# The four query tiles of the opening attention head get a later planned landing time

## The chip, the cores and the metric

The kernel runs on one core of one Trainium2 chip. The metric is the device time in microseconds (us) of one execution. The profile names the engines: PE (TensorE matmul) with its weight loads PEld, DVE (VectorE), ACT (ScalarE), POOL (GpSimd) and SP (SyncE, which issues every DMA of this kernel; SPq is its queue).

## The reference, cut to what matters

One layer over 2048 prompt frames and 64 sample frames. An input projection (1024 to 6144 columns) gives queries, keys, values and gates of two branches; branch A is the differential attention in which the change lies:

```python
s = jnp.einsum('bqhcd,bkhcd->bhcqk', q, k).astype(jnp.float32) * (DK_A ** -0.5)
s = s - slopes[None, :, None, None, None] * dist[None, None, None]
s = jnp.where(allowed[None, None, None], s, -jnp.inf)
p = jax.nn.softmax(s, axis=-1)
a = p[:, :, 0] - lam * p[:, :, 1]
return jnp.einsum('bhqk,bkhe->bqhe', a.astype(v.dtype), v)
```

There are 4 heads. Branch B is a chunkwise retention. Both are normalised, gated, projected and added to the input.

## The kernel before, in words

**Stages.** The prompt is taken in two halves of 1024 frames. For each half the projection runs (the "w stream"), and while its later columns are still being multiplied, attention over that half runs beside it (the "z stream"): for each of 4 heads, and for each query tile of 256 frames (p = 0 to 3 in the first half, 4 to 7 in the second), scores Q K (lines 1879 and 1880), a mask and a minimum (1888), exponentials (1919), transposes (1991) and the product with V (1969 to 1971). Products are made of high and low float32r parts, which is why three matmuls stand where one would be expected. Retention blocks (2336 and on) run as a third stream.

**The order is planned by hand.** The Python program is itself a scheduler. `Hybrid.loop` holds a set of generators with priorities and a clock `self.pe`; each matmul moves this clock by its columns / 2.4 + 13 ns (`P`), and a generator that yields a time is resumed when the clock has reached it. PE, ACT and DVE execute their instructions in exactly the order in which the generators wrote them. The planned times are in no instruction: they only decide the order. Where the plan finds nothing to do, its clock jumps, and no instruction stands for the gap.

**Loads.** `ld` (line 279) issues a DMA on SP and returns the time at which the plan counts the data as landed: a running DMA clock that takes 1 ns for every 300 bytes, plus `DMA_LAT` = 2600 ns. A query tile is four DMAs of 131,072 bytes: 4 x 437 ns = 1.75 us on that clock; a weight tile of 262,144 bytes takes 0.87 us.

**The opening head.** `h_loader` calls `load_head(0, 0)`, which loads the two K tiles of head 0, its query tile p = 0, and, 3000 ns of the plan later, p = 1; 2000 ns after that the table `dfar`, and then V. The pool `q` has two buffers, so `q_loader` can load p = 2 only when p = 0 has been used, and p = 3 when p = 1 has; the load of p = 3 also waits until the K of head 1 is loaded (`self.heads` is not empty), `CALM` = 18000 ns after the end of `load_head(0, 0)`. `attn_head` takes the tiles in order and yields each one's planned landing time `tq` (line 1855) before it writes the scores. Line 1791 adds `FIRSTQ` = 4000 ns to the planned landing of tile p = 0 of head 0. All other query tiles count as landed when `ld` says so.

**What fills the wait.** While `attn_head` sleeps, lower priorities are written. At this place the w stream is in the first product of the second half (`transposed`, line 1426, with `mm_group`, line 1137): for two row tiles, two groups of 256 columns and two of 288, each group 8 steps of 3 matmuls; `mm_group` yields after each step. Then come the values of the second half (`natural`, 512 columns wide, 8 steps of 3 for each frame tile), whose weights pass from a load (`ws`) through a cast on ACT (`wh`, line 727) and a subtraction on POOL (`wl`, line 748).

Of the kernel before, what the change touches and what calls it, by code (L numbers as in the profile page):

```python
# [44 lines left out]
FIRSTQ = 4000.0  # L45
# [127 lines left out]
class Hybrid:  # L173
# [1595 lines left out]
    def load_head(self, half, h):  # L1769
        ap = self.ap  # L1770
        nu = half + 1
        ks = [[None] * nu for _ in range(2)]
        vs = [[None] * nu for _ in range(2)]
        tk = tv = 0
        for u in range(nu):
            usl = slice(1024 * u, 1024 * u + 1024)
            for c in range(2):
                yield from self.take("K")
                k = self.sb(ap, [128, 1024], "K", dt=F32R)
                for j in range(2):  # L1780
                    o = 64 * (j ^ c)
                    tk = self.ld(k[o:o + 64].bitcast(F32), self.kT[j][h, 64 * c:64 * c + 64, usl], 1 << 18)
                ks[c][u] = k
        hd = {"ks": ks, "vs": vs, "tk": tk, "tv": None}
        if self.far:
            self.heads.append(hd)
        else:
            self.far = True
            yield from self.load_q(0, 0)
            q, t = self.qs[0]  # L1790
            self.qs[0] = q, t + FIRSTQ
            yield self.pe + 3000
            yield from self.load_q(0, 1)
            yield self.pe + 2000
            self.ld(self.dfar, self.i["c_dfar"], 1 << 19)
            self.heads.append(hd)
        for u in range(nu):
            usl = slice(1024 * u, 1024 * u + 1024)
            for j in range(2):
                yield from self.take("V")  # L1800
                v = self.sb(ap, [128, 8, 128], "V", dt=F32R)
                tv = self.ld(v.bitcast(F32), self.vN[j][usl, 128 * h:128 * h + 128]
                             .rearrange("(t p) e -> p t e", p=128), 1 << 19)
                vs[j][u] = v
        hd["tv"] = tv

    def load_q(self, h, p):
        t0 = 256 * p
        yield from self.take("q")
        q = self.sb(self.ap, [128, 4, 256], "q", dt=F32R)  # L1810
        for j in range(2):
            qj = self.qT[j][h, :, t0:t0 + 256].rearrange("(c d) t -> d c t", c=2)
            for o in (0, 64):
                t = self.ld(q[o:o + 64, 2 * j:2 * j + 2].bitcast(F32), qj, 1 << 17)
        self.qs.append((q, t))

    def q_loader(self, half):
        for h in range(4):
# [1383 lines left out]
```

## Time and profile before

| | us |
|---|---|
| median of 3 runs | 1899.02 (1897.36 to 1899.72) |
| the profiled execution, device time | 1898.9 |
| its span, first to last instruction | 1897.1 |
| PE busy | 1872.0 |
| DVE, ACT, POOL busy | 1332.9, 972.9, 673.1 |
| mean granted TensorE clock | 0.999 |

A row of the timeline reads: start, length, engine, line, operation, output <- inputs, shapes, count, and in brackets how long the engine was idle just before and what released it. Matmuls overlap, so the length of one is more than the distance to the next. A row of the waits reads: who waited <- for whom: us in total, times, longest.

### The profile page before, as it was taken

The page shows a single profiled execution, that of the slowest core. Times are in us where ns is not written, and L with a number is a line of the kernel's source. Part 1 is how long each engine was busy: PE and PEld are TensorE (multiplying, and loading weights), DVE is VectorE, ACT ScalarE, POOL GpSimd, SP SyncE. Part 2 cuts the span into 40 slices and gives each one's busy share as a digit, 9 for nine tenths or more (in the row PEclk, how much of TensorE's full clock was granted, in tenths as well). Part 3 has the DMA queues.
Part 4 walks back from the last instruction along what each step waited for, and adds up shares of the span by engine and source line. Part 5 has one row for each costly group of instructions (what it writes and reads, how often), then busy time and mean ns, then how long its engine had stood idle before and what let it go on. Part 6 is the DMA issues. An engine that isn't in the chain of part 4 may idle for free.

```text
span 1897.1 us, 33035 instructions
## 1 busy us (share of the span) xinstructions
PE 1872.0 (99%) x11090; PEld 1648.1 (87%) x11090; DVE 1332.9 (70%) x3111; ACT 972.9 (51%) x2266; POOL 673.1 (35%) x729
## 2 busy tenths in 40 slices
PE   9999999999998999999999999999999999999999
PEld 7788778888887889888888899989999999999887
DVE  6765757657584777886467686588886869977664
ACT  6434544555434665655455565456666536654221
POOL 2420355555552122121311344332122546522442
PEclk9999999999999999999999999999999999999999
DMA  7664555666857867554622854945534899976542
GB/s 259 209 178 125 162 154 182 180 197 193 250 181 198 225 187 195 160 171 125 181 73 76 231 138 128 238 127 141 142 103 140 266 250 285 274 233 204 174 156 78
DMA packets 402556, 340.09 MB, mean 179 GB/s; under 512 B 85329, under 2 KB 348625, under 8 KB 401362
## 3 DMA queue, kind: packets, MB, share of 16 engines
q1 hardware_dynamic: 402386, 337.97, 61.0%
q8 instruction: 88, 1.44, 0.3%
q14 instruction: 82, 0.67, 0.1%
HBM read 218.27 MB, written 118.75 MB: 178 GB/s over the span
## 4 chain that ended last, share of the span: by engine, by line
PE 89%; DVE 4%; DMA 4%; SPq 1%; ACT 1%; issue 1%; POOL 0%; DVEq 0%; POOLq 0%; ACTq 0%
PE mm L1137 29%; PE mm L989 8%; PE tp L989 4%; PE at L1991 3%; PE s L1880 2%; PE s L1879 2%; PE s L989 2%; PE mm L1564 2%; PE pv L1971 2%; PE pv L1970 2%; PE pv L1969 2%; DMA q<-qT 1%; PE s L2793 1%; PE s L2795 1%; PE s L2794 1%; PE pv L2257 1%
## 5 line engine op out<-in xcount | busy, mean ns | idle before, releaser
L748 POOL TENSOR_TENSOR wl<-ws,wh 128x512 fp32r<-128x512 f32 x108 | 148.6, 1387 | 244.3 <-ACT wh L727 233.5
L1137 PE MATMUL mm<-wh,xh 128*128 128x512 f32 x504 | 203.7, 404 | 0.0
L1137 PE MATMUL mm<-wl,xh 128*128 128x512 f32 x504 | 197.8, 393 | 0.8 <-POOL wl L748 0.8
L1137 PE MATMUL mm<-wh,xl 128*128 128x512 f32 x504 | 198.2, 393 | 0.0
L1137 PE MATMUL mm<-xh,wh 128*128 128x288 f32 (+2 forms) x544 | 180.2, 331 | 0.0
L1137 PE MATMUL mm<-xl,wh 128*128 128x288 f32 (+2 forms) x544 | 176.1, 324 | 0.0
L1137 PE MATMUL mm<-xh,wl 128*128 128x288 f32 (+2 forms) x544 | 176.1, 324 | 0.0
L1919 ACT ACTIVATE row<-row,a_mx 128x1024 f32<-128x1024 f32 (+7 forms) x144 | 150.1, 1044 | 9.5 <-DVE a_mx L1898 9.5
L2007 DVE TENSOR_TENSOR atl<-at,ath 128x512 fp32r<-128x512 f32 (+1 forms) x144 | 93.1, 658 | 76.1 <-ACT ath L2005 75.6
L2005 ACT CAST ath<-at 128x512 fp32r<-128x512 f32 (+1 forms) x144 | 79.0, 564 | 108.0 <-PE at L1991 102.1
L856 POOL TENSOR_TENSOR wl<-ws,wh 128x256 fp32r<-128x256 f32 x64 | 54.5, 852 | 195.7 <-ACT wh L847 195.6
L1888 DVE CUSTOM_DVE_ANT_0 row<-s,dfar 128x512 f32<-128x512 f32 (+2 forms) x151 | 92.8, 629 | 38.1 <-PE s L1880 37.6
L1745 POOL TENSOR_TENSOR r_y<-r_y,r_sq 128x256 f32<-128x256 f32 x32 | 28.2, 881 | 253.6 <-DVE r_sq L1742 215.5
L1137 PEld LDWEIGHTS mm<-wh,xl 128*128 128x128 f32 x504 | 94.7, 188 | 21.7
L1137 PEld LDWEIGHTS mm<-wl,xh 128*128 128x128 f32 x504 | 95.1, 189 | 18.4 <-POOL wl L748 1.1
L1137 PEld LDWEIGHTS mm<-wh,xh 128*128 128x128 f32 x504 | 94.9, 188 | 17.4 <-DVE raw L1308 0.2
L1137 PEld LDWEIGHTS mm<-xh,wh 128*128 128x128 f32 x544 | 103.1, 190 | 7.2
L1137 PEld LDWEIGHTS mm<-xl,wh 128*128 128x128 f32 x544 | 103.2, 190 | 7.0
L1137 PEld LDWEIGHTS mm<-xh,wl 128*128 128x128 f32 x544 | 102.9, 189 | 6.7
L1941 DVE SCALAR_TENSOR_TENSOR row<-row,a_w 128x1024 f32<-128x1024 f32 (+5 forms) x88 | 101.4, 1158 | 0.0
L1879 PE MATMUL s<-K,q 128*128 128x512 f32 (+3 forms) x243 | 91.8, 379 | 0.6 <-DMA q<-qT 0.4
L1880 PE MATMUL s<-K,q 128*128 128x512 f32 (+3 forms) x243 | 88.3, 365 | 0.9 <-DMA q<-qT 0.9
(543 smaller groups left out, 6044.3 us busy)
## 6 DMA issues: line engine op xcount, KB each, us to landing
ws<-in_w_in_dram SPq DMA_DIRECT2D x155, 256.0 KB, 3.5
q<-qT SPq DMA_DIRECT2D x128, 128.0 KB, 3.1
K<-kT SPq DMA_DIRECT2D x48, 256.0 KB, 4.4
V<-vN SPq DMA_DIRECT2D x24, 512.0 KB, 5.5
row<-in_x_prompt_dram SPq DMA_DIRECT2D x16, 512.0 KB, 4.7
wz<-in_w_in_dram SPq DMA_DIRECT2D x32, 256.0 KB, 4.2
row<-in_cache_k_T_dram SPq DMA_DIRECT2D x32, 256.0 KB, 3.2
row<-in_cache_v_diff_dram SPq DMA_DIRECT2D x32, 256.0 KB, 3.4
```

The costliest lines, as they stand in the source:

```text
L748: eng.tensor_sub(l, st, h.bitcast(F32))
L856: nc.gpsimd.tensor_sub(l[:, cs], src, h[:, cs].bitcast(F32))
L989: nc.tensor.matmul(ps, w[:, c], xs[x][c], start=bool(tag) and c == 0 and i == 0, stop=c == 3 and i == 2, skip_group_check=True)
L1137: nc.tensor.matmul(ps, p, q, start=c == 0 and i == 0, stop=c == KC - 1 and i == 2)
L1879: nc.tensor.matmul(ps, q1s, kk, start=True, stop=False)
L1880: nc.tensor.matmul(ps, q2s, kk, start=False, stop=True)
L1888: nc.vector.tensor_tensor_reduce(out=row[:, k0:k0 + n], in0=ps, in1=tab, scale=-SLOPES[h], scalar=3.0e38, op0=ALU.add, op1=ALU.min, accum_ ...
L1919: nc.scalar.activation(u, u, AF.Exp, bias=mx, scale=-1.0, accum_out=lp[:, k:k + 1])
L1941: nc.vector.scalar_tensor_tensor(out=u0, in0=u1, scalar=w[:, 0:1], in1=u0, op0=ALU.mult, op1=ALU.add)
L1991: nc.tensor.transpose(at[:, w:w + 128], src, self.ident)
L2005: nc.scalar.copy(ah[:, :w], at[:, :w])
L2007: nc.vector.tensor_sub(al[:, :w], at[:, :w], ah[:, :w].bitcast(F32))
```

## The change

The planned landing time of the query tiles is altered in one place and not in another. `load_head` no longer adds `FIRSTQ` to the first tile; `load_q` adds it to every tile with h = 0 and p below 4, that is to the four tiles of head 0 in the first half. For p = 0 the sum is as before; p = 1, 2 and 3 count as landing 4000 ns later. No instruction is added or removed.

```diff
@@ load_head
             self.far = True
             yield from self.load_q(0, 0)
-            q, t = self.qs[0]
-            self.qs[0] = q, t + FIRSTQ
             yield self.pe + 3000
             yield from self.load_q(0, 1)
             yield self.pe + 2000
@@ load_q
             for o in (0, 64):
                 t = self.ld(q[o:o + 64, 2 * j:2 * j + 2].bitcast(F32), qj, 1 << 17)
-        self.qs.append((q, t))
+        self.qs.append((q, t if h or p > 3 else t + FIRSTQ))
```

## The prediction

> **What bounds the kernel now.** I read the page first:
>
> ```profile
> span 1897.1 us, 33035 instructions
> ...
> PE 1872.0 (99%) x11090; PEld 1648.1 (87%) x11090; DVE 1332.9 (70%) x3111; ACT 972.9 (51%) x2266; POOL 673.1 (35%) x729
> ```
>
> PE is busy for all but 25.1 us, and the change removes no PE work. It can only win idle PE time or a slow clock, or make more of them. So next the waits of PE, those for query tiles and the one for POOL in that place:
>
> ```profile
> PE tp L1879 <- DMA q<-qT: 3.8, 1, 3.8
> PE tp L1880 <- DMA q<-qT: 1.5, 2, 1.1
> PE s L1880 <- DMA q<-qT: 0.9, 2, 0.6
> PE mm L1137 <- POOL wl L748: 0.8, 1, 0.8
> PE s L1879 <- DMA q<-qT: 0.4, 1, 0.4
> ```
>
> Query tiles cost 6.6 us in all. The PE timeline shows where (the first row is the last score matmul of tile p = 0):
>
> ```profile
> 605.29 0.28 PE L1880 MATMUL s<-K,q 128*128 128x256 f32 x1
> 605.96 0.41 PE L1879 MATMUL s<-K,q 128*128 128x384 f32 x1 [0.39 <-DMA q<-qT]
> 606.96 0.41 PE L1880 MATMUL s<-K,q 128*128 128x384 f32 x1 [0.59 <-DMA q<-qT]
> ...
> 608.89 0.29 PE L1137 MATMUL mm<-xh,wh 128*128 128x288 f32 x1
> ...
> 611.56 0.29 PE L1137 MATMUL mm<-xh,wl 128*128 128x288 f32 x1
> 615.64 0.35 PE L1879 MATMUL tp<-K,q 128*128 128x256 f32 x1 [3.79 <-DMA q<-qT]
> 616.48 0.35 PE L1880 MATMUL tp<-K,q 128*128 128x256 f32 x1 [0.49 <-DMA q<-qT]
> ...
> 617.41 0.44 PE L1137 MATMUL mm<-xh,wh 128*128 128x288 f32 x1
> ...
> 620.29 0.38 PE L1137 MATMUL mm<-xh,wh 128*128 128x288 f32 x1
> 631.70 0.34 PE L1879 MATMUL s<-K,q 128*128 128x384 f32 x1
> ```
>
> Tile p = 1 (384 and 512 keys wide) costs 0.39 + 0.59 = 0.98 us, p = 2 (from 615.64) 3.79 + 0.49 = 4.28. The row at 631.70 is p = 3, without a wait. Then I asked for stretches (busy PE, PEld, DVE, ACT, POOL; granted clock; DMA share; GB/s):
>
> ```profile
> 617.40:620.30 2.90, 2.90 (x14) 2.90 (x14) 2.17 (x10) 0.40 (x1) 0.00 (x0) 0.50 0.75 162
> 726.00:862.00 136.00, 136.00 (x875) 122.77 (x874) 108.12 (x319) 79.09 (x204) 26.79 (x23) 1.00 0.59 169
> ```
>
> After the long wait the granted clock is 0.50 for 2.9 us. The 12 matmuls from 617.41 to 620.29 take 0.24 us each; the 20 from 608.89 to 611.56 took 0.1335. That is 12 x 0.1065 = 1.28 us by rows, 1.45 by clock (2.90 x 0.50); I take 1.4. So the place has 0.98 + 4.28 + 1.4 = 6.7 us to win, 7.0 with the 0.3 that tile p = 0 waits (the 0.9 in the third row of the waits less the 0.59 of p = 1), which the change leaves alone.
>
> The Trainium skill ("TensorE: Matmul & The Clock Gate", Part 1) says that an idle window of about 3.4 us halves the clock and that about 3.4 us of work restores it; the trace agrees, with 4.28 us of waiting and 2.9 us at 0.50.
>
> **The change part by part.** Nothing is removed or added on any engine; four DMAs for each tile stay. What moves is the place of the scores of p = 1, 2, 3 in PE's order (with their DVE and ACT work), against the w stream's steps.
>
> *Tile p = 0*: same due time, so same place. It costs nothing.
>
> *Tile p = 1.* Call D the plan's landing of p = 0 without the 4.0. Between the two tiles SP issued one weight tile, so p = 1 lands at D + 0.87 + 1.75 = D + 2.62:
>
> ```profile
> 596.49 2.55 SPq L280 DMA_DIRECT2D q<-qT  x4
> 599.14 0.54 SPq L280 DMA_DIRECT2D ws<-in_w_in_dram  x1
> 599.73 3.18 SPq L280 DMA_DIRECT2D q<-qT  x4
> ...
> 605.89 2.94 SPq L285 DMA_DIRECT2D qbT<-ev  x1
> ...
> 609.41 1.68 SPq L285 DMA_DIRECT2D qbT<-ev  x3
> 611.20 2.53 SPq L280 DMA_DIRECT2D q<-qT  x4
> ...
> 614.88 1.75 SPq L280 DMA_DIRECT2D K<-kT  x3
> 619.51 0.81 SPq L285 DMA_DIRECT2D qbT<-ev  x2
> ...
> 622.18 3.33 SPq L280 DMA_DIRECT2D q<-qT  x4
> ```
>
> Before, p = 0 is due at D + 4.0, is written up to one step (3 x 0.1335 = 0.40 us) later, and takes 1.36 in the plan (8 score matmuls at 0.12 and one step). It ends at D + 5.4 to 5.8, when p = 1 is overdue: no step between them. After, p = 1 is due at D + 6.62: 0.9 to 1.2 us, three steps. On the chip PE comes to p = 1 at 606.8 instead of 605.57 (605.29 + 0.28). The two halves of the tile were there at 605.96 and 606.96, so its 0.98 us of waiting go.
>
> *Tile p = 2.* Its load is written right after p = 0, so nothing is put ahead of it on SP, which in the rows above issues with hardly a gap up to 611.20. I take the halves to land as before, 615.64 and 616.48. Before, the plan waited for it for the 21 matmuls from 608.89 to 611.56, 2.8 us. Its due time is now 4.0 later and p = 1 ends 1.2 later: 2.8 + 4.0 - 1.2 = 5.6 us, 14 steps. Are there so many? From 605.57 to 624.05:
>
> ```profile
> L1137 PE MATMUL mm<-xh,wh 128*128 128x288 f32 x18 | 6.0, 332 | 0.0
> ```
>
> 18 steps: 3 before p = 1, one within it, 14 before p = 2. It just suffices, and these matmuls have their weights. On the chip: p = 1 took 608.89 - 605.57 - 0.98 = 2.34 us, so 606.8 + 2.34 + 5.6 = 614.7. PE then waits 0.9 and 0.5 us, 1.4 instead of 4.28: 2.9 won.
>
> *The clock.* 1.4 us of waiting in two parts stands nearer to the 1.06 of a later tile than to 4.28:
>
> ```profile
> 724.08 0.41 PE L1880 MATMUL tp<-K,q 128*128 128x384 f32 x1 [1.06 <-DMA q<-qT]
> ...
> 724.00:726.00 2.00, 1.92 (x12) 1.87 (x13) 1.47 (x6) 0.00 (x0) 0.00 (x0) 1.00 0.79 172
> ```
>
> There the clock stayed at 1.00. So the 1.4 us of slow clock go too; if not, they stay in the sum (bounds 0 and 1.4; I take 1.4). By the same section of the skill, 1.4 us is under its window, so no drop; the sum would be the same.
>
> *Tile p = 3.* It had no wait to lose, and its 4.0 us can only cost. Its load was issued at 622.18 and landed 5.0 to 6.0 us after each issue:
>
> ```profile
> DMA to landing us min/median/max: 5.0/5.1/6.0
> ...
> SPq L285 <- ACT ev L1591: 4.4, 2, 2.8
> ```
>
> The first half was there at 628.2, the scores came 3.5 us later. PE is now 5 us ahead: at 626.5 if the order around it were as before. SP stood 2.9 us before the stores of 619.51 (614.88 + 1.75 to 619.51; 2.8 in the second row, from SP's own waits), for the ACT copy of a group that PE finished late because of the stall; that group now ends before p = 2, so the load can come up to 2.8 earlier and land at 625.4. Wait: 0 to 1.7 us. The 0.8 us for POOL's `wl` lies in the same stretch and can vanish or grow: -0.8 to +1. I take 0.3 lost for both.
>
> *Later.* The attention of head 0 ends up to 4 us later in the plan. What is behind it on PE is covered by the w stream: from 726 to 862, where the first half's attention ends, PE has no idle time. The second half's query loads begin at 906.5, so the two streams meet again there:
>
> ```profile
> 862.17 0.39 PE L1879 MATMUL s<-K,q 128*128 128x512 f32 x1
> ...
> L280 SPq DMA_DIRECT2D q<-qT x16: 573/598/609, 906.5 to 980.5; - x16
> ```
>
> I cost it at nothing; without that cover it is the third rival.
>
> *Sum.* 0.98 + 2.9 + 1.4 - 0.3 = 5.0 us. From 1898.9, the profiled execution's time, that is 1893.9; the median of the runs is 0.1 higher, so **1894.0**.
>
> **The rivals.**
>
> *The w stream runs dry.* The ten steps (14 + 3 against 7) that now stand before p = 2 stood after it, and gave POOL time for the `wl` parts of the 512-wide values:
>
> ```profile
> 621.03 2.55 POOL L748 TENSOR_TENSOR wl<-ws,wh 128x512 fp32r<-128x512 f32 x2 [24.10 <-ACT wh L727]
> ```
>
> For it: POOL takes 1.3 us for each weight tile, PE 0.7 for the three matmuls on it (512 / 2.4 + 13 ns each, as the plan counts). Against it: POOL had waited 24.1 us for a cast that waits until PE has left the old weights; these steps come earlier, so the casts do. If the cover is lost, ten steps, 4.0 us, are given back: 1893.9 + 4.0 + 0.1 = 1898.0.
>
> *The load of p = 2 slips.* If SP gets the stores of the finished group ahead of it, it follows their ACT copy, and PE stalls as before. Of the sum only the 0.98 is left, so 1898.0 as well. Against it: the load is written before the group ends. In this case the change does not do what it says.
>
> *Head 2 gives it back, and more.* The wait at 724.08 is behind weight loads that wait for POOL (a row of SP's timeline, then two of the waits there):
>
> ```profile
> 698.96 10.49 SPq L280 DMA_DIRECT2D ws<-in_w_in_dram  x5
> SPq L280 <- POOL wl L748: 9.9, 6, 3.8
> ACT thi L1384 <- PE mm L1137: 4.3, 3, 2.6
> ```
>
> If this chain keeps its time while PE comes 5.0 us sooner, 1.06 becomes 6.1 and the clock falls for another 1.4: 1893.9 + 5.0 + 1.4 + 0.1 = 1900.4, slower. It decides from 1.4 + 5.0 of extra wait in one place on; twice such a place gives 1906.8. Against it: the third row, ACT between its casts waits for PE, so the chain follows PE.
>
> **How the numbers follow.** The forecast has 0.58, the dry w stream 0.20, the slipped load 0.08, head 2 (or a second place like it) 0.14. About 0.2%, 3.8 us, is what can be told from no change: under 1895.2 is faster, over 1902.8 slower. The forecast is faster; the first two rivals and 0.06 of the third are within; the rest, 0.08, is slower. The forecast's own range is 1891.2 (all 7.0 us and the 0.8) to 1895.2; to 1899.6 it takes in the first two rivals and leaves out head 2.
>
> **What would show it.** Right: 18 matmul steps (x18) before the first scores of p = 2, the waits of p = 1 gone, that of p = 2 near 1.4, clock 1.00 from 617 to 621, p = 3 with under 1.7 us. Wrong: p = 2 loaded later than 611.2 (slipped), a POOL wait of some us at line 1137 before 640 (dry), or a new wait for q, K or V after 640 of more than 1.1 us (head 2). It would be wrong in size if the clock still fell.

## The result, and the profile after

The changed kernel takes 1897.16 us (median of 14 runs, 1894.36 to 1899.80) beside 1899.68 for the kernel before on the same chip (14 runs, 1897.36 to 1904.96). The ratio is 0.9983, 95% interval 0.9975 to 0.9991: 3.2 us faster, between 1.7 and 4.75. Predicted were 5.0 us. The median is 3.2 us above the forecast of 1894.0 and outside the forecast's own range (1891.2 to 1895.2). It lies in the wider range up to 1899.6, which the prediction gave to its first two rivals, and in the part called "within 0.2%". In the changed file every line from 1791 on has a number lower by two, so the scores are lines 1877 and 1878 there.

The page of the changed kernel, span and busy times first:

```profile
span 1893.1 us, 33045 instructions
...
PE 1869.9 (99%) x11090; PEld 1647.9 (87%) x11090; DVE 1341.6 (71%) x3111; ACT 973.9 (51%) x2266; POOL 670.9 (35%) x729
```

The span is 4.0 us shorter: PE is busy for 2.1 us less and idle for 1.9 us less. The ten instructions more than before are semaphore instructions; the counts of work are the same. The PE timeline of the changed kernel around the opening head (the columns are those of the prediction; in brackets the idle time just before and what ended it):

```profile
605.89 0.33 PE L1877 MATMUL s<-K,q 128*128 128x384 f32 x1
606.24 0.41 PE L1878 MATMUL s<-K,q 128*128 128x384 f32 x1
...
613.95 0.29 PE L1137 MATMUL mm<-xh,wl 128*128 128x288 f32 x1
615.74 0.35 PE L1877 MATMUL tp<-K,q 128*128 128x256 f32 x1 [1.50 <-DMA q<-qT]
616.86 0.35 PE L1878 MATMUL tp<-K,q 128*128 128x256 f32 x1 [0.77 <-DMA q<-qT]
...
627.43 0.38 PE L2014 MATMUL pv<-ident,a_e 128*1 128x128 f32 x2
630.81 0.50 PE L1137 MATMUL mm<-wh,xh 128*128 128x512 f32 x1 [2.99 <-ACT wh L727]
632.15 0.80 PE L1137 MATMUL mm<-wl,xh 128*128 128x512 f32 x1 [0.85 <-POOL wl L748]
...
636.12 0.34 PE L1877 MATMUL s<-K,q 128*128 128x384 f32 x1
```

Tile p = 1 (605.89) waits no more. Tile p = 2 waits 1.50 + 0.77 = 2.27 us where it waited 4.28. But 14 us later stands a stall that the kernel before did not have: 2.99 us for the high part of a weight tile of the values, then 0.85 for its low part (0.77 before). The scores of p = 3 (636.12) come without a wait, 4.4 us later than before (631.70). Stretches of the changed kernel (length, then busy time and count of PE, PEld, DVE, ACT and POOL, then granted clock, DMA share and GB/s):

```profile
617.00:621.00 4.00, 4.00 (x26) 3.62 (x27) 3.05 (x13) 1.57 (x4) 0.00 (x0) 1.00 0.89 215
632.00:636.00 4.00, 3.85 (x14) 3.26 (x15) 1.40 (x3) 1.53 (x3) 0.10 (x1) 0.57 1.11 290
640.00:726.00 86.00, 86.00 (x534) 76.28 (x533) 64.73 (x190) 55.39 (x137) 19.46 (x17) 1.00 0.69 204
```

After tile p = 2 the clock stays at 1.00; after the new stall it is 0.57 over 4 us, which costs 3.85 x 0.43 = 1.7 us. That is as much as the slow stretch of the kernel before costs, 3.42 x 0.50 = 1.7 us:

```profile
617.05:620.47 3.42, 3.42 (x16) 3.42 (x15) 2.52 (x12) 0.54 (x2) 0.00 (x0) 0.50 0.80 180
```

From 640 to 726 PE has no idle time at all in the changed kernel. In the kernel before, the same stretch and the waits in it were:

```profile
640.00:726.00 86.00, 83.56 (x508) 73.38 (x508) 65.65 (x199) 54.23 (x138) 18.24 (x15) 1.00 0.68 196
```

```profile
PE tp L1880 <- DMA q<-qT: 1.1, 1, 1.1
PE tp L1720 <- DVE r_lo L1714: 0.9, 1, 0.9
PE pv L1971 <- DVE atl L2007: 0.4, 1, 0.4
```

So idle time plus slow clock from 600 to 640 is 6.4 + 1.7 = 8.1 us before and 6.1 + 1.7 = 7.8 after. **The place that the change aims at has gained next to nothing**; the 2.4 us of waits that are gone lie after it.

Why is the weight late? SP's timeline of the changed kernel, and the cast that waited for the load:

```profile
610.50 3.85 SPq L280 DMA_DIRECT2D q<-qT  x4
...
616.49 2.39 SPq L280 DMA_DIRECT2D K<-kT  x4
618.92 1.21 SPq L280 DMA_DIRECT2D V<-vN  x2
620.23 4.98 SPq L280 DMA_DIRECT2D q<-qT  x4
625.31 0.54 SPq L280 DMA_DIRECT2D ws<-in_w_in_dram  x1
```

```profile
630.14 0.62 ACT L727 CAST wh<-ws 128x512 fp32r<-128x512 f32 x1 [2.53 <-DMA ws<-in_w_in_dram]
```

In the kernel before, the load was issued at about the same time. PE came to the same place in its work, the eighth 512-wide step of the values, only at 634.45 (SP's timeline, then PE's):

```profile
625.60 1.01 SPq L280 DMA_DIRECT2D ws<-in_w_in_dram  x2
```

```profile
634.45 0.39 PE L1137 MATMUL mm<-wh,xh 128*128 128x512 f32 x1
```

After the change PE is there at 627.8 (630.81 less the 2.99). The load stands on SP behind K, V and the query tile p = 3 (616.49 to 625.21). SP began p = 3 two us earlier than before, but the first of its four DMAs held SP for 3.03 us where it had taken 1.37 (the kernel before, then the changed one), so the weight behind it was issued only 0.3 us earlier:

```profile
622.18 1.37 SPq L280 DMA_DIRECT2D q<-qT  x1
```

```profile
620.23 3.03 SPq L280 DMA_DIRECT2D q<-qT  x1
```

One more milestone is used below: the last transpose of the second half's queries (line 1340), here in the kernel before and in the changed one (first and last start are the two times):

```profile
L1340 PE MATMUL tp<-ident,raw x136: 222/272/331, 83.6 to 937.6; 128*128 128x128 f32 x128, 64*128 64x64 f32 x8
```

```profile
L1340 PE MATMUL tp<-ident,raw x136: 222/272/329, 84.1 to 933.5; 128*128 128x128 f32 x128, 64*128 64x64 f32 x8
```

From the first score to this transpose it takes 937.6 - 603.5 = 334.1 us before and 933.5 - 603.2 = 330.3 after; from the transpose to the end of the span 959.5 and 959.6. Nearly the whole gain of the two profiles (3.8 of 4.0 us) lies in the first interval.

### The profile page after: what moved, and what is told of

The parts are those of the page before. It is cut to its first block, busy times and chain, and to the rows that moved or that the text cites. A ratio compares the mean times of both kernels' runs of the same rounds, so it can differ in the third digit from the quotient of the medians.

```text
span 1893.1 us, 33045 instructions
## 1 busy us (share of the span) xinstructions
PE 1869.9 (99%) x11090; PEld 1647.9 (87%) x11090; DVE 1341.6 (71%) x3111; ACT 973.9 (51%) x2266; POOL 670.9 (35%) x729
## 4 chain that ended last, share of the span: by engine, by line
PE 86%; DMA 6%; DVE 4%; SPq 1%; ACT 1%; issue 1%; POOL 1%; DVEq 0%; ACTq 0%; POOLq 0%
PE mm L1137 27%; PE mm L989 8%; PE tp L989 4%; PE at L1989 3%; PE s L1877 2%; PE s L1878 2%; PE s L989 2%; PE pv L1969 2%; PE pv L1968 2%; PE pv L1967 2%; PE mm L1564 2%; PE s L2793 1%; PE s L2791 1%; PE s L2792 1%; SPq L280 1%
## 5 line engine op out<-in xcount | busy, mean ns | idle before, releaser
L1877 PE MATMUL s<-K,q 128*128 128x512 f32 (+3 forms) x241 | 91.7, 381 | 0.2 <-DVE a_acc L1886 0.2
L727 ACT CAST wh<-ws 128x512 fp32r<-128x512 f32 x111 | 66.9, 617 | 41.0 <-DMA ws<-in_w_in_dram 11.2
```

Source lines behind the costliest of these rows:

```text
L727: self.nc.scalar.copy(h, st)
L1877: nc.tensor.matmul(ps, q1s, kk, start=True, stop=False)
```

## The experiments

Two theories stood against each other: that the time is decided by what is won and lost at the opening head (A in the expectations), and that it is decided by how the order written after it happens to fall (B). All ratios are to the kernel before on the same chip. "Lost" is idle PE time plus time lost to a lower clock, summed over whole windows of 4 us; since it multiplies mean values of a window, it has 7.9 for the 8.1 us above.

| kernel | ratio, 95% interval | lost 600 to 640 | lost 640 to 1252 | lost 1432 to 1600 | first score to milestone |
|---|---|---|---|---|---|
| before | 1 | 7.9 | 5.4 | 5.7 | 334.1 |
| changed | 0.9983, 0.9975 to 0.9991 | 7.8 | 4.0 | 5.0 | 330.3 |
| e1, p = 0, 2 | 0.9991, 0.9982 to 1.0000 | 7.9 | 6.7 | 5.3 | 336.1 |
| e2, p = 0, 1, 2 | 1.0008, 1.0000 to 1.0017 | 5.2 | 9.5 | 6.4 | 333.7 |
| e3, p = 0, 3 | 0.9990, 0.9981 to 0.9999 | 8.3 | 1.9 | 5.7 | 331.9 |
| e4, one weight first | 0.9998, 0.9989 to 1.0006 | 3.4 | 2.3 | 13.3 | 327.9 |
| e5, the same in before | 1.0000, 0.9991 to 1.0009 | 7.9 | 8.7 | 6.0 | 337.5 |
| e6, three weights first | 1.0012, 1.0003 to 1.0021 | 3.6 | 4.3 | 12.3 | 322.7 |
| e7, 4400 ns | 1.0013, 1.0004 to 1.0021 | 9.7 | 7.0 | 6.8 | 332.2 |
| e8, 3600 ns | 1.0007, 0.9995 to 1.0020 | 7.9 | 5.6 | 8.7 | 337.0 |
| e9, changed again | 0.9983, 0.9974 to 0.9992 | 7.5 | 5.1 | 5.3 | 330.4 |
| e10, 3600 ns again | 0.9993, 0.9984 to 1.0002 | 7.5 | 5.1 | 6.5 | 337.0 |

### One tile at a time

**e1**: the margin for p = 0 and 2 only.

```diff
-        self.qs.append((q, t if h or p > 3 else t + FIRSTQ))
+        self.qs.append((q, t + FIRSTQ if not h and p in (0, 2) else t))
```

> The 4.0 us of margin for tiles p = 0 and p = 2 of the opening head alone; p = 1 and p = 3 count as landing when the load says so. Theory A (the change takes out the waits for p = 1 and p = 2, and the w stream gives most of it back at 628 to 632, where a weight tile of the 512-wide values is loaded behind K, V and the tile p = 3): p = 1 waits 0.98 as before, p = 2 waits about 2, the wait for that weight stays near 3 to 4 us, ratio about 0.998 to 0.999. Theory B (the local place gives nothing net, and the gain comes from the stretch 640 to 726, because p = 3 and what follows it move): no gain without p = 3 late, ratio 1.000, idle PE in 640 to 726 near 2.4 us.

Measured 0.9991. The long wait of p = 2 is down to 0.75 + 0.35 us, yet as much is lost from 600 to 640 as before: p = 3 comes early and waits 0.56 and 0.89, and the clock falls. The wait for the weight's high part, which theory A put at 3 to 4 us, did not come, and 4.4 us are lost from 640 to 726. The interval of the ratio takes in what both theories expected.

**e2**: for p = 0, 1 and 2.

```diff
-        self.qs.append((q, t if h or p > 3 else t + FIRSTQ))
+        self.qs.append((q, t + FIRSTQ if not h and p in (0, 1, 2) else t))
```

> The margin for p = 0, 1 and 2; p = 3 counts as landing when the load says so. Theory A: as the changed kernel, ratio 0.997 to 0.999; p = 1 without a wait, p = 2 about 2.3, the weight of the values about 3.8 us. Theory B: the idle PE in 640 to 726 comes back (2.4 us), ratio near 1.000.

Measured 1.0008. It has the smallest loss at the head of these three (5.2) and the longest time: 4.1 us more are lost between 640 and 1252 than in the kernel before. Waits of PE there, 726 to 950 and then 950 to 1250:

```profile
PE s L1878 <- DMA q<-qT: 1.2, 1, 1.2
PE s L1877 <- DMA q<-qT: 0.7, 1, 0.7
...
PE s L2334 <- DMA row<-qbT: 3.6, 1, 3.6
PE at L1989 <- DVE atl L2005: 1.2, 1, 1.2
```

They are waits of the next heads and of retention, not those of 640 to 726 that the expectation of theory B named: nothing is lost there. At the head, the 3.8 us at the weight that theory A expected did not come either: PE stood at p = 3 first, for 0.64 + 0.79 us. Neither theory gave this.

**e3**: for p = 0 and 3, so that the plan counts p = 1 and 2 as landing when it did before.

```diff
-        self.qs.append((q, t if h or p > 3 else t + FIRSTQ))
+        self.qs.append((q, t + FIRSTQ if not h and p in (0, 3) else t))
```

> The margin for p = 0 and p = 3 alone. Theory A: p = 1 waits 0.98 and p = 2 4.28 with 2.9 us at half the clock, as before; ratio 1.000. Theory B: the same local waits, but idle PE in 640 to 726 under 0.5 us in place of 2.4, ratio about 0.9985.

Measured 0.9990, with 8.3 us lost at the head. The waits are not quite those expected: the clock falls already at p = 1, PE comes later to p = 2 and waits 2.04 + 0.54 us there, and the clock falls again. From 640 to 726 only 0.1 us are lost, as theory B expected. The kernel that does not fill the wait of p = 2 is as fast as the one that does (e1). That speaks for B.

### The new stall alone

**e4**: the changed kernel, with the K and V of the next head 1000 ns later in the plan, so that the values' weight tile is written ahead of them on SP.

```diff
-                yield self.pe + CALM
+                yield self.pe + CALM + 1000
```

> The changed kernel, and the K and V of head 1 are loaded 1000 ns of the plan later, so that one weight tile of the 512-wide values stands on SP ahead of them and of the tile p = 3 in place of behind them. Theory A: the wait of 2.99 + 0.85 us at that weight goes, and the 2 to 3 us at half the clock after it: 4 to 5 us faster than the changed kernel, less up to 1.5 us of a new wait for p = 3; ratio 0.995 to 0.997. Theory B, or a w stream that is held by POOL and not by the load: the wait stays at 3 us or more, ratio 0.998 to 1.000.

SP's timeline of e4, in which the weight now stands ahead of K, V and p = 3:

```profile
615.77 0.38 SPq L280 DMA_DIRECT2D ws<-in_w_in_dram  x1
616.20 2.39 SPq L280 DMA_DIRECT2D K<-kT  x4
618.63 1.21 SPq L280 DMA_DIRECT2D V<-vN  x2
619.94 5.79 SPq L280 DMA_DIRECT2D q<-qT  x4
```

The wait for `wh` is gone, that for `wl` too, and the clock stays up: 3.4 us are lost at the head instead of 7.8. **The stall's cause is shown.** The total is no better for it: 0.9998. Attention ends earlier (the last score begins at 1415.9, in the changed kernel at 1422.3), and then 8 us more are lost than in the changed kernel. The stretch of the changed kernel, that of e4, and the waits of PE in that of e4:

```profile
1430.00:1600.00 170.00, 164.97 (x1317) 162.87 (x1316) 133.02 (x226) 91.82 (x199) 87.42 (x69) 1.00 0.82 240
```

```profile
1430.00:1600.00 170.00, 158.45 (x1244) 156.66 (x1244) 126.11 (x214) 84.39 (x180) 80.79 (x64) 0.98 0.81 233
```

```profile
PE tp L1719 <- DVE u L1584: 3.4, 1, 3.4
PE at L1564 <- DVE ev L1584: 2.6, 1, 2.6
PE mm L1564 <- DVE ev L1584: 2.0, 2, 1.4
PE s L1564 <- DVE ev L1584: 1.6, 1, 1.6
```

DVE's own idle time there, in the changed kernel and in e4:

```profile
L1584 DVE TENSOR_TENSOR ev<-mm,u 128x288 f32<-128x288 f32 (+1 forms) x17 | 7.5, 440 | 5.1 <-DMA gbT<-ev 2.3 <-PE mm L1564 2.0 <-DMA gaT<-ev 0.8
```

```profile
L1584 DVE TENSOR_TENSOR ev<-mm,u 128x288 f32<-128x288 f32 (+1 forms) x16 | 6.9, 439 | 10.6 <-DMA gbT<-ev 7.0 <-PE mm L1564 3.6
```

These sums of line 1584 wait until the gates' stores (`gbT`) have emptied a buffer: 7.0 us instead of 2.3. Why the stores are later for them is not shown.

**e5**: the same edit in the kernel before, where PE does not wait for the high part of a weight.

> The kernel before, with only the K and V of head 1 loaded 1000 ns of the plan later, so that one weight tile of the values stands ahead of the last K part, V and the tile p = 3. It has no margins for p = 1 to 3. If the two stalls are bound together as I think (the waits for p = 1 and p = 2 first, the weight second), the first stays whole (0.98 and 4.28 us and the half clock, 6.5 to 7 us in all) and the weight costs nothing here: first-half interval (first scores to the last transpose of line 1340) within 2 us of before, ratio 0.999 to 1.001. If the order of the weight alone is worth something, that interval falls by 4 us or more.

Measured 1.0000, with as much lost at the head as before (7.9): the earlier weight is worth nothing where PE does not come early. The interval to the milestone missed what was expected: 337.5 us, 3.4 longer than before, with 8.7 lost from 640 to 1252.

**e6**: the changed kernel with the same 1000 ns made 3500.

```diff
-                yield self.pe + CALM
+                yield self.pe + CALM + 3500
```

> The changed kernel, with K and V of head 1 3500 ns of the plan later: three weight tiles ahead of them. Local theory: no wait at the weight, as with one tile ahead; p = 3 lands 1.7 us later still (two more weight tiles of 0.87) and may wait 0 to 2 us; idle and half clock from 600 to 640 together 3 to 5 us against 7.8 in the changed kernel. If the 6 us that the run with one tile ahead lost after 1430 belong to finishing attention sooner, they come back here (idle 1430 to 1600 over 9 us, ratio about 1.000); if they are a matter of how the later order falls, they need not (5 to 6 us, ratio about 0.997).

Measured 1.0012. First score to milestone takes 322.7 us, the least of all; after 1430 12.3 us are lost, for the same engine:

```profile
PE s L1564 <- DVE ev L1584: 5.0, 3, 1.9
PE s L1564 <- DVE xl L1529: 3.7, 2, 1.9
```

So the gain ends behind 1430 in a second order too. That it ends there because attention finishes sooner is not shown: e5 begins its last score as early as e6 (1419.8 and 1420.3) and loses 6.0 us there, not 12.3.

### The size of the margin

**e7** and **e8**: 4400 and 3600 ns for p = 1, 2, 3, with 4000 kept for p = 0.

```diff
-        self.qs.append((q, t if h or p > 3 else t + FIRSTQ))
+        self.qs.append((q, t if h or p > 3 else t + FIRSTQ + (400.0 if p else 0.0)))
```

```diff
-        self.qs.append((q, t if h or p > 3 else t + FIRSTQ))
+        self.qs.append((q, t if h or p > 3 else t + FIRSTQ - (400.0 if p else 0.0)))
```

> The changed kernel with 4400 in place of 4000 ns for p = 1, 2 and 3. The local places should stay: p = 2 waits 1.8 to 2.3 us, the weight 3 to 4. If the gain from 640 to 726 and after is a mechanism, the ratio stays at 0.998; if it is how the order falls, the ratio moves by 0.001 or more for these 0.4 us and the first-half interval by 2 us or more.

> The same with 3600 ns: p = 2 waits 2.3 to 2.7 us, the weight 3 to 4; the same two readings of the ratio and the first-half interval as with 4400.

Measured 1.0013 and 1.0007. Both have the weight stall of the changed kernel (2.8 and 3.3 us for `wh`). In e8, p = 1 waits 0.52 us again and p = 2 only 0.89 + 0.53, where 2.3 to 2.7 were expected. What e7 has in addition is a fall of the clock behind p = 2, where the changed kernel's stayed at 1.00. Its PE timeline and the stretch behind it:

```profile
615.70 0.35 PE L1877 MATMUL tp<-K,q 128*128 128x256 f32 x1 [1.35 <-DMA q<-qT]
616.68 0.35 PE L1878 MATMUL tp<-K,q 128*128 128x256 f32 x1 [0.63 <-DMA q<-qT]
```

```profile
617.30:620.70 3.40, 3.40 (x15) 3.04 (x14) 1.86 (x8) 0.06 (x1) 0.00 (x0) 0.52 0.91 198
```

A wait of 1.35 + 0.63 us brought the clock to 0.52 in e7; one of 1.50 + 0.77 did not lower it in the changed kernel. The last section says why.

**e9** and **e10**: the changed kernel and e8 once more, on one chip.

> The changed kernel once more, as it stands, beside the next kernel on one chip. If its gain belongs to the order that its 4000 ns give, it repeats: ratio to the kernel before 0.9975 to 0.9991. If the gain was noise of the runs, the ratio lies above 0.9991.

> The margin of 3600 ns for p = 1, 2, 3 once more, on the same chip. If the margin itself were worth the gain, nine tenths of it would be worth nearly the same: ratio 0.998 to 0.9995. If what counts is how the later order falls, it repeats its first result: ratio 1.0000 to 1.0015, at least 0.001 above the changed kernel in the same call.

e9 repeats its 0.9983. e10 gives 0.9993, where 1.0000 to 1.0015 was expected of a repeat; the two results of this kernel are 0.0014 apart. It is 0.0010 above the changed kernel in the same call, just the least that was expected, with intervals that overlap. So 3600 ns stands near no change, and the difference to 4000 ns is probable rather than shown. At the head the two executions of this kernel differ: e10 waited only 1.17 us for `wh`, and its clock fell behind p = 2.

The milestone stands at 933.9, 939.9 and 938.7 in e9, e8 and e10, the first scores at 603.5, 602.9 and 601.7. So the interval is 330.4 (330.3 the first time) and 337.0 both times: in these two pairs it belongs to the order and repeats within 0.1 us. The rest of the span does not: in the two executions of the 3600 ns kernel it takes 1898.4 - 939.9 = 958.5 and 1893.4 - 938.7 = 954.7 us. That is the scatter in which gains of 2 us disappear.

## Why the prediction was right and wrong

- **p = 1, right.** Three steps stand before it, its 0.98 us are gone.
- **p = 2, right in kind, 0.9 us too much.** 18 steps stand between p = 0 and the scores of p = 2, as counted, and PE is free for them at 614.2 (predicted 614.7). The wait left is 2.27, not 1.4: the prediction took the halves to land at 615.64 and 616.48 as before, but SP, 0.7 us earlier at it (610.50), took 3.85 us for the four DMAs instead of 2.53, and they were there at 615.74 and 616.86. Won: 2.0, not 2.9.
- **The clock there, right by luck.** It stayed at 1.00 from 617 to 621. The prediction judged by the length of the wait, but e7 lost the clock after a shorter one (1.98 us for 2.27). The size was low too: the slow stretch of before lasts from 617.05 to 620.47, not 2.9 us, so 1.7 us were won and not 1.4. The last section shows why a wait of this length can lower the clock or not.
- **The term that failed: "Wait: 0 to 1.7 us ... I take 0.3 lost for both".** It priced p = 3 and POOL's `wl`. p = 3 waited for nothing, because PE came to it later still (636.12). (Its first half consists of two DMAs and had landed at 628.7 in the kernel before, not at 628.2.) What stood in its place is the weight tile in front: 2.99 + 0.85 us, less the 0.77 of before, and 1.7 us of slow clock, together 4.8 instead of 0.3. SP did come 2 us earlier to p = 3, as the working said, but its first DMA held SP until 623.26, so that the weight behind it gained nothing. The working asked only whether POOL is in time for the 512-wide values, and not whether the load before the cast is. The rows were at hand: SP busy with K, V and p = 3 until 625.6, and a PE that would be 5 us early. The rival "the w stream runs dry" had the place and nearly the price (4.0), and the wrong reason. What the prediction held against it, that the casts come earlier where the steps do, is what failed: e4 shows that the cast was held by the order of SP's queue.
- **"Later ... I cost it at nothing", wrong in the other direction.** From 640 to 726 the 2.4 us of before are gone: PE came to these places at another time. That they go is not owed to the filled wait: they are gone in e2 and e3 too, and with 1.0008 and 0.9990 the one is slower and the other faster than before.
- **The sum.** By the terms as measured: 0.36 (p = 0 does not wait in this execution) + 0.98 + 2.0 + 1.7 - 4.8 = 0.2 us won at the head, and 2.4 from 640 to 726. The interval from first score to milestone is 3.8 us shorter; the 1.1 or so that are missing are busy PE time, which the traces assign to no place. That the total came within 2 us of the 5.0 is luck: an error of 4.5 us one way met gains that were in no term.
- **The other rivals.** The load of p = 2 did not slip (610.50, before 611.20). Head 2 gave nothing back: the 1.06 us at 724 went, and no wait for q, K or V follows before 950.

What is settled: the mechanism at the head, the new stall and its cause, that in e4 and e6 its removal brought nothing in total and the waits for DVE after 1430 grew, and that the changed kernel's gain repeats. What stays open is why just this order loses less from 640 on, and why those waits grow. e1, e2, e7, e8 and e10, which also shorten the wait of p = 2 or fill it, lie from 0.9991 to 1.0013, none of them with an interval wholly under 1.0000. So I read the 0.17% as a property of this one order and not as the worth of the later landing time. The intervals to the milestone are no measure of equal work between different orders, since each may leave other work for later. No kernel tried beat the changed one.

## What to carry to other kernels

Where a hand-planned order moves work in front of a late load, price the loads behind that work too: PE's order moves forward, a queue that is busy with other loads does not, and the first tile behind it becomes the next stall. Judge such a change by the sum of losses over a stretch that holds both the old stall and the next, and then by whether a neighbouring margin gives the same; if a tenth more turns the sign, what was measured is an order, not a rule. A wait that is removed can come back as other waits in a later stage (here those for DVE and the gates' stores, in e4 and e6), so the whole time decides.

## What was not expected of the hardware

**The length of a wait does not tell whether the clock falls.** In e3 two short waits were enough (its PE timeline, then the stretch behind):

```profile
605.52 0.41 PE L1877 MATMUL s<-K,q 128*128 128x384 f32 x1 [0.51 <-DVE a_acc L1886]
606.40 0.41 PE L1878 MATMUL s<-K,q 128*128 128x384 f32 x1 [0.47 <-DMA q<-qT]
```

```profile
606.70:610.20 3.50, 3.50 (x13) 3.11 (x12) 2.51 (x10) 0.71 (x2) 0.00 (x0) 0.51 1.15 318
```

0.98 us of waiting in two parts (p = 0 had waited 0.35 us just before) cost 3.5 x 0.49 = 1.7 us of clock, more than these waits; in the kernel before, 0.39 + 0.59 at the same place (0.36 before them) left it at 1.00:

```profile
607.00:610.50 3.50, 3.50 (x23) 3.32 (x24) 3.02 (x15) 1.72 (x6) 0.00 (x0) 1.00 1.14 330
```

The clock's own records show what decides. In the twelve traces, a slow stretch before the last 100 us lasts 3.41 us or twice that, and within one trace its edges are whole multiples of 3.413 us apart. The two falls of e3, at 606.72 and 616.96, are 3 x 3.413 us apart; two falls of e8, at 632.05 and 939.25, are 90 x 3.413. If the first 1800 us of each trace are cut into pieces of 3.413 us that fit these edges, there are 26 falls from 1.00. No piece with less than 1.2 us of idle PE time was followed by one, and every piece with more than 1.92 us was; in between there are both. So a wait counts by what falls into one piece. Of e10's 1.54 + 0.79 us, 2.11 us of idle time lie in one piece, and the next is slow:

```profile
613.39:616.80 3.41, 1.30 (x8) 1.16 (x9) 1.03 (x4) 0.41 (x1) 2.11 (x2) 1.00 0.62 171
616.80:620.21 3.41, 3.41 (x16) 3.04 (x15) 1.53 (x6) 0.40 (x1) 0.00 (x0) 0.50 0.98 232
```

In the changed kernel an edge at 615.10 divides nearly the same wait (1.50 + 0.77) into 0.86 and 1.40 us, and no fall follows:

```profile
611.69:615.10 3.41, 2.55 (x20) 2.32 (x18) 1.01 (x4) 2.51 (x7) 2.64 (x3) 1.00 0.80 237
615.10:618.52 3.42, 2.02 (x11) 1.74 (x12) 1.27 (x5) 0.00 (x0) 1.10 (x1) 1.00 0.64 173
```

The pair e3 and before lies at the lower end: 1.22 us of idle time in the piece before the fall (603.31 to 606.72), 1.18 in the piece from 603.40 to 606.81 of the kernel before. The Trainium skill ("TensorE: Matmul & The Clock Gate", Part 1) speaks of one idle window of about 3.4 us, and of a window that runs freely, so that the cost depends on its phase. The second agrees with these rows; of the first they show that PE need not be idle that long without a break. What decides between 1.2 and 1.92 us stays open.

**The same four DMAs hold SP for different times.** A query tile took 2.53 and 3.33 us to issue in the kernel before, 3.85 and 4.98 in the changed one and 5.79 in e4, with no sign of it in the share of busy DMA engines (603.5 to 617: 1.07 in the kernel before, 0.98 in the changed one). For p = 3 the excess lies in the first of the four: 1.37 us in the kernel before, 3.03 in the changed one and 3.83 in e4, while the others take 0.60 to 0.61 each. All three stand right behind the two loads of V. The trace lists these holds as waits for PE (2.3 us in the changed kernel), but the scores of p = 1, whose buffer the load takes, were done at 608.3, so their cause stays open. A plan that counts 1.75 us for it is most wrong just where loads stand close together.
